# A hybrid two-layer decoder trunk on one core: other look-ups in PEER, wide u products throughout, an un-normed first third in the conv mixer, and an earlier split of an output slab

## The chip, the cores and the metric

One core of one Trainium2 chip. The metric is the time of one execution in microseconds of device time, and the median over several runs stands for a kernel. Engines are named as in the profile: PE (TensorE matmuls; PEld its weight loads), DVE (VectorE), ACT (ScalarE), POOL (GpSimd), SP (SyncE, which issues the transfers).

## What is computed

256 tokens of width 1024 pass two layers: a gated short convolution or an attention, each followed by a PEER expert retrieval, with a norm ahead of each and one at the end.

```python
def reference(x, ...):
    for i in range(DEPTH):                      # DEPTH = 2
        hn = rms_norm(x, norm_mix[i])
        if i % N_MIXERS == 0:
            x = x + short_conv_mixer(hn, conv_w_in[j], conv_w[j], conv_w_out[j])
        else:
            x = x + moba_mixer(hn, attn_w_qkv[j], attn_w_o[j])
        x = x + peer_ffn(rms_norm(x, norm_ffn[i]), peer_w_q[i], peer_k1[i], peer_k2[i], peer_u[i], peer_v[i])
    return rms_norm(x, norm_final)

def short_conv_mixer(h, w_in, conv_w, w_out):
    b_gate, c_gate, z = jnp.split(h @ w_in, 3, axis=-1)
    ...                                         # causal convolution of c_gate * z, width 3
    return (b_gate * u_conv) @ w_out

# peer_ffn, per chunk of 128 tokens, 8 heads
        v1, i1 = lax.top_k(s1, PEER_TOPK)       # 16 of 128 keys, twice
        v2, i2 = lax.top_k(s2, PEER_TOPK)
        top_s, top_pos = lax.top_k(cand, PEER_TOPK)     # 16 of the 256 sums
        e_idx = jnp.take_along_axis(cidx, top_pos, axis=-1)
        g = jax.nn.softmax(top_s, axis=-1)
        a = jax.nn.gelu(jnp.einsum('td,thkd->thk', xc, u_emb[e_idx]), approximate=False)
        return jnp.einsum('thk,thkd->td', g * a, v_emb[e_idx])
```

All values are float32; the 16384 experts of a layer have one row in u_emb and one in v_emb.

## The kernel before, in words

The order of the work on every engine is written out by hand. All weights pass as a row of tiles ("items") of 128x1024: 24 of conv_w_in in the order c gate, z, b gate, 8 of conv_w_out, then for layer 0's PEER 8 of w_q, 128 of u and 128 of v, then the same for the second layer with 24 of attn_w_qkv and 8 of attn_w_o. Three buffers each hold an item raw, split into a rounded part `hi` (ACT, L171) and the rest `lo` (DVE or POOL, L176); `halved` names the items whose POOL split runs as two halves. The activations are split alike (XH, XL), and each product is the sum of hi·XH, hi·XL and lo·XH. `issue` starts an item's transfer on SP as soon as the item three places ahead of it is split; `prefetch(n)` transposes u items to n+3 (DVE, L157) and splits to n+2 ahead of item n's matmuls (`next_item`).

PEER multiplies with all 16384 rows of u and v. A u item gives 128 rows for 256 tokens; from item WIDE on, hi multiplies XH and XL as one operand of 512 columns (L965) into a whole bank, ACT copies one half out (L1144), DVE adds the other (`both`, L1134) and ACT applies the gelu; below WIDE = 16, three products of 256 columns (L967, L968, L971) sum up in half a bank. Four banks are used in turn, so item k+4 waits for the add of item k's pair.

Beside the first 64 u items, DVE makes the look-ups from a list of side work: `add(cost, ...)` puts one operation on it, and after each item `run_side(1.62)` issues as many as the saved-up credit pays for; `pause()` ends a round. Per half of the tokens (i = 0, 1): top-k of the scores and of the sums, then for each of 128 picks its two key numbers, by comparing the pick's row and column with thresholds (`is_ge`, `is_equal` into `hot`), multiplying by the table `vp` and summing over 16 places, with folds (`fold`, L1029) by 8, 4 and 2 and a last add. The side list has line L215 for all that is called through `add`. Later side work (L1174, L1182, L1196) turns the list into gates.

The start: x is loaded, its squares summed, the norm applied, x transposed on PE and split, and only then the 8 c-gate items are multiplied (`mm_wstat`, L545), then z and b gate. Dummy matmuls (`warm`, L299) keep PE at work meanwhile. After the last b-gate item, DVE multiplies the gated result (L683), ACT rounds it (L684) and the 8 conv_w_out items follow (L558); the second of these is split on POOL. In attention, the v third begins with two items taken together, bank by bank (`mm_bank`, L565 to L567).

## Time and profile before

| what | value |
|---|---|
| median of 3 runs | 1809.76 us (1808.52 to 1813.9) |
| the profiled execution | 1812.88 us, of which its span is 1811.1 us |
| busy: PE, DVE, ACT, POOL | 99%, 76%, 50%, 39% of the span |
| granted clock of PE, mean | 0.995 of 2.4 GHz |
| read from HBM | 315.83 MB, 176 GB/s over the span |
| chain that ended last | PE 87%, DVE 7%, DMA 3% |

The busy share says how long an engine had some instruction in flight. Since matmuls overlap, PE's share stays near 100% where it issues more slowly too; its pace is read from the starts of its instructions.

### The profile page before, as it was taken

Reading aid. Unit: us, or ns where it says so; the run is one execution under the profiler, and the core shown is the slowest. Engines: PE = TensorE matmul, PEld = TensorE weight load, DVE = VectorE, ACT = ScalarE, POOL = GpSimd, SP = SyncE. Lnnn points to the kernel's source line nnn. Section 1 sums busy time; section 2 is a strip of 40 time slices with the busy share of each in tenths; the row PEclk is TensorE's granted clock in tenths of the full one; section 3 lists DMA queues with packets and bytes.
Section 4 is the critical chain, followed back from the end, with each engine's and each line's share of the span. In section 5 each row is a group of like instructions: output and inputs, shape, how many; then the busy total and the mean of one; then the engine's idle time right before and its main releaser. Section 6 shows DMA issues by size and latency. Waiting matters only on the chain.

```text
span 1811.1 us, 30954 instructions
## 1 busy us (share of the span) xinstructions
PE 1791.1 (99%) x11217; PEld 1536.6 (85%) x11217; DVE 1370.7 (76%) x2251; ACT 906.8 (50%) x1153; POOL 700.2 (39%) x553
## 2 busy tenths in 40 slices
PE   9999999999999999999999999999999999999998
PEld 8979988888888888888878799888888888888886
DVE  4648899888888887555566488998888898875555
ACT  5455555554554444544454555565455544445443
POOL 1047888888720000000220388988888200000000
PEclk9999999999999999999999999999999999999999
DMA  7566566656556556766562665665565565657664
GB/s 206 157 196 197 167 176 174 187 166 176 171 157 182 168 171 185 228 193 196 172 181 83 174 198 168 182 179 174 172 175 164 158 186 169 176 176 230 193 193 138
DMA packets 204576, 321.06 MB, mean 177 GB/s; under 512 B 26221, under 2 KB 157317, under 8 KB 203910
## 3 DMA queue, kind: packets, MB, share of 16 engines
q1 hardware_dynamic: 202006, 312.33, 58.4%
q10 hardware_dynamic: 2416, 6.75, 1.1%
q8 instruction: 88, 1.44, 0.3%
q14 instruction: 66, 0.54, 0.1%
HBM read 315.83 MB, written 3.15 MB: 176 GB/s over the span
## 4 chain that ended last, share of the span: by engine, by line
PE 87%; DVE 7%; DMA 3%; issue 1%; ACT 1%; POOL 1%; SPq 1%; DVEq 0%; ACTq 0%; POOLq 0%
PE psum L558 40%; PE psum L965 19%; PE psum L971 11%; PE psum L1189 4%; PE psum L545 3%; DVE tr L157 2%; DVE big L215 2%; PE psum L968 2%; PE psum L967 2%; PE psum L591 2%; DMA raw<-in_peer_u_dram 1%; DVE lo L176 1%; PE psum L1003 1%; POOL lo L176 1%; PE psum L567 1%
## 5 line engine op out<-in xcount | busy, mean ns | idle before, releaser
L176 POOL TENSOR_TENSOR lo<-tr,hi 128x512 fp32r<-128x512 f32 x496 | 632.5, 1310 | 120.1 <-ACT hi L171 120.1
L171 ACT ACTIVATE hi<-raw 128x1024 fp32r<-128x1024 f32 x331 | 350.0, 1060 | 452.4 <-PE psum L558 362.7
L176 DVE TENSOR_TENSOR lo<-raw,hi 128x1024 fp32r<-128x1024 f32 x312 | 382.7, 1228 | 253.6 <-ACT hi L171 247.4
L558 PE MATMUL psum<-hi,x 128*128 128x512 f32 x2208 | 553.2, 392 | 0.7 <-ACT hi L171 0.7
L558 PEld LDWEIGHTS psum<-hi,x 128*128 128x128 f32 x2208 | 409.0, 188 | 82.6 <-ACT hi L171 1.1
L965 PE MATMUL psum<-x,hi 128*128 128x512 f32 x1792 | 458.9, 397 | 5.2 <-DVE big L1134 5.2
L965 PEld LDWEIGHTS psum<-x,hi 128*128 128x128 f32 x1792 | 323.2, 190 | 64.6 <-issue 4.2
L157 DVE STREAM_TRANSPOSE tr<-raw 128x1024 f32<-128x1024 f32 x256 | 315.6, 1233 | 43.2 <-DMA raw<-in_peer_u_dram 26.6
L171 ACT ACTIVATE hi<-tr 128x1024 fp32r<-128x1024 f32 x256 | 270.7, 1059 | 144.5 <-DVE tr L157 134.1
L558 PE MATMUL psum<-lo,x 128*128 128x512 f32 x1104 | 295.1, 389 | 0.4 <-POOL lo L176 0.4
L971 PEld LDWEIGHTS psum<-x,lo 128*128 128x128 f32 x2048 | 279.5, 191 | 18.0 <-POOL lo L176 0.2
L176 POOL TENSOR_TENSOR lo<-raw,hi 128x1024 fp32r<-128x1024 f32 (+1 forms) x31 | 58.3, 1904 | 599.7 <-ACT hi L171 558.1
L971 PE MATMUL psum<-x,lo 128*128 128x256 f32 x2048 | 289.2, 283 | 0.0
L558 PEld LDWEIGHTS psum<-lo,x 128*128 128x128 f32 x1104 | 207.1, 188 | 43.8 <-POOL lo L176 0.8
L1144 ACT ACTIVATE big<-psum 128x512 f32<-128x512 f32 x112 | 66.8, 596 | 165.6 <-PE psum L971 165.4
L1289 POOL TENSOR_TENSOR big<-xbuf,big 128x256 f32<-128x256 f32 x2 | 1.4, 732 | 383.4 <-DVE rstd L348 383.4
L1134 DVE TENSOR_TENSOR big<-psum,big 128x512 f32<-128x512 f32 x112 | 77.2, 689 | 72.3 <-ACT big L1144 72.0
L1174 DVE TENSOR_TENSOR xbuf<-psum,eT 128x1536 f16<-128x1536 f16 x128 | 119.8, 936 | 10.2 <-PE psum L1189 10.2
L1196 DVE SCALAR_TENSOR_TENSOR big<-psum,big 128x512 f32<-128x512 f32 x128 | 86.5, 677 | 3.1 <-PE psum L1189 3.1
L1182 DVE TENSOR_TENSOR xbuf<-xbuf,psum 128x1024 f16<-128x1024 f16 x128 | 85.8, 671 | 1.3
L1189 PEld LDWEIGHTS <-xbuf 128*128 128x128 f16 x2048 | 68.5, 97 | 19.5 <-issue 15.7
L1189 PE MATMUL psum<-xbuf 128*128 128x64 f16 x2048 | 83.7, 193 | 0.0
(173 smaller groups left out, 1451.0 us busy)
## 6 DMA issues: line engine op xcount, KB each, us to landing
raw<-in_peer_u_dram SPq DMA_DIRECT2D x1024, 128.0 KB, 2.9
raw<-in_peer_v_dram SPq DMA_DIRECT2D x256, 512.0 KB, 3.7
raw<-in_conv_w_in_dram SPq DMA_DIRECT2D x96, 128.0 KB, 2.7
raw<-in_attn_w_qkv_dram SPq DMA_DIRECT2D x96, 128.0 KB, 2.6
raw<-in_peer_w_q_dram SPq DMA_DIRECT2D x64, 128.0 KB, 3.1
raw<-in_conv_w_out_dram SPq DMA_DIRECT2D x8, 512.0 KB, 3.9
raw<-in_attn_w_o_dram SPq DMA_DIRECT2D x8, 512.0 KB, 3.6
x_dram<-xbuf ACTq DMA_DIRECT2D x2, 1024.0 KB, 4.8
```

What stands on the lines that cost most here:

```text
L157: dve.transpose(TR[m % 3].rearrange("p b (g i) -> p g b i", g=4), RAW[m % 3].rearrange("p (g m) -> p g m", m=256))
L171: act.activation(HI[m % 3], src, AF.Copy)
L176: eng.tensor_sub(LO[m % 3][:, c], src[:, c], HI[m % 3][:, c])
L558: pe.matmul(banks[j], x[:, j // 2 * 128:j // 2 * 128 + 128], w[:, j % 2 * 512:j % 2 * 512 + 512], start=(first and p == 0), stop=(last and ...
L965: pe.matmul(o, w, X2[:, b], start=(b == 0), stop=False, skip_group_check=True)
L971: pe.matmul(o[:, 0:256], lo[:, b * 128:b * 128 + 128], XH[:, b], start=False, stop=(b == 7), skip_group_check=(o.shape[-1] == 512))
L1134: dve.tensor_tensor(a, halves(k, 0), a, op=OP.add)
L1144: act.activation(A[:, k - 1:k + 1], halves(k, 1), AF.Copy)
L1174: dve.tensor_tensor(HOT[s % 2].rearrange("p b (r k) t -> p b r k t", r=3), numbers[:, None, None].to_broadcast([128, TOK // 2, 3, 64, 2]), ...
L1182: dve.tensor_tensor(OHG[s % 2], one_hot[:, None].to_broadcast([128, 2, TOK // 2, 64, 2]), gate_rows[:, s, :, :, None, :].to_broadcast([128 ...
L1189: pe.matmul(o, pairs[:, t // 2, :, t % 2], OHG[s % 2][:, a, t // 2, :, t % 2], start=(a == 0), stop=(a == 1))
L1196: dve.scalar_tensor_tensor(w, banks[s % 3].rearrange("p (t k) -> p k t", k=64), 1.0 / GSC, w, op0=OP.mult, op1=OP.mult)
```

## The change

- **Wide u products:** WIDE is 0 in both layers, so all u items take the 512-column form.
- **Look-ups:** tables hold each entry once, not twice; the places of a pick lie side by side in `hot`, the compares (`hits`) write pairs, and two TENSOR_REDUCE in place of three folds and an add form the sums. The 128x128 subtract and others that read two operands from SBUF get one of them through PSUM. Costs on the side list change, and a `pause()` follows.
- **First third of the conv:** x is transposed un-normed, scaled by the gain on the way out of PSUM (`chunk`), and multiplied with the c-gate items. The token factors come later (`norm_behind`), as a row R that two matmuls spread; the eight chunks are rescaled for the z and b thirds (`normed`), and the c gate gets R when it leaves PSUM. Half of x is loaded on ACT's queue ahead of the weights, the other half on SP's behind three items.
- **Second output slab:** its split is called behind the first gated copy.
- **Attention:** two more items are split in halves.

```diff
-WIDE = (16, 16)
+WIDE = (0, 0)
...
     def load_x(i, h):
-        c = slice(h * 512, h * 512 + 512)
-        sp.dma_start(x_in[:, i * D + h * 512:i * D + h * 512 + 512], x[0, i * 128:(i + 1) * 128, c])
+        (sp if h else act).dma_start(x_in[:, (2 * h + i) * 512:(2 * h + i) * 512 + 512].rearrange("p (q r) -> p q r", q=4),
+                     x[0, i * 128:(i + 1) * 128].rearrange("p (q r) -> p q r", q=4)[:, :, 128 * h:128 * h + 128])
...
-    warm(WARM)
-    spread_gain(hi4[2:4])
+    warm(WARM - 8)
+    gT = sb.tile([128, 8], F32, name="gT")
+    pe.transpose(lo4[3][:, 0:8], gr8, ident[0:8, 0:8])
+    dve.tensor_copy(gT, lo4[3][:, 0:8])
+    warm(11)
...
+    def chunk(c):
+        bk = hi4[c % 4][:, c // 4 * 256:c // 4 * 256 + 256]
+        for i in range(2):
+            pe.transpose(bk[:, i * 128:i * 128 + 128], XT[i][:, c * 128:c * 128 + 128], ident)
+        act.activation(XH[:, c], bk, AF.Copy, scale=gT[:, c:c + 1])
+        dve.scalar_tensor_tensor(XL[:, c], bk, gT[:, c:c + 1], XH[:, c], op0=OP.mult, op1=OP.subtract)
+    def normed(c):
+        v = scratch(3 * D + c % 2 * 256, 256)
+        pool.tensor_tensor(v, XH[:, c].bitcast(F32), XL[:, c].bitcast(F32), op=OP.add)
+        dve.tensor_tensor(v, v, R, op=OP.mult)
+        act.activation(XH[:, c], v, AF.Copy)
+        dve.tensor_sub(XL[:, c], v, XH[:, c])
     def norm_in():
...
+        for i in range(2):
+            kept(i, 0)
+        chunk(0)
         split_to(0)
+        for c in (1, 2, 3):
+            chunk(c)
+        warm(4)
+    def norm_behind(b):
+        if b == 1:
+            for i in range(2):
+                kept(i, 1)
+                squares(i, 0)
+                begun(i)
+        elif b == 2:
+            for c in range(4, 8):
+                chunk(c)
+        elif b == 3:
...
+            for i in range(2):
+                root(i)
+                dve.tensor_scalar(scratch(i * 128, 128), ident, rstd[:, i:i + 1], -0.5, op0=OP.mult, op1=OP.mult)
+            late_consts()
+        elif b == 4:
+            for i in range(2):
+                pe.matmul(hi4[0][:, i * 128:i * 128 + 128], ones, scratch(i * 128, 128), start=True, stop=True)
+            load_gain(norm_ffn, 0)
+            load_keys(0)
+        elif b > 4:
+            if b == 5:
+                dve.tensor_copy(R, hi4[0][:, 0:256])
+            normed(b - 5)
...
             next_item(mm_wstat(lo4, b), 1.0)
+            norm_behind(b)
         drain_side()
-        for j in range(4):
-            act.activation(cT[:, 2 * j:2 * j + 2].rearrange("p c t -> p (c t)"), lo4[j], AF.Copy)
         for b in range(8):
             next_item(mm_wstat(hi4, b))
+            if b < 5:
+                normed(b + 3)
+            if 1 < b < 6:
+                s = slice(2 * b - 4, 2 * b - 2)
+                dve.tensor_tensor(cT[:, s], lo4[b - 2].rearrange("p (c t) -> p c t", t=256),
+                                  R[:, None].to_broadcast([128, 2, 256]), op=OP.mult)
...
             if j:
                 out_lo(j - 1)
+            else:
+                split_to(n + 1)
...
                 on_pool.update(range(n + 15, n + 20))
+                halved.update((n + 16, n + 17))
...
+        def hits(i, c, ends, op):
+            dve.tensor_tensor(hot[i][:, 8 * c:8 * c + 8].rearrange("p h n (a r) -> p (h n) a r", r=2),
+                              picks[:, c, :, None].to_broadcast([128, 128, 8, 2]),
+                              ends.rearrange("p (a r) -> p a r", r=2)[:, None].to_broadcast([128, 128, 8, 2]), op=op)
...
-            add(0.5, dve.tensor_tensor, gg[:, i], ts[:, i], ts[:, i, :, 0:1].to_broadcast([128, 8, 16]),
+            add(0.3, dve.tensor_copy, side1, ts[:, i])
+            add(0.3, dve.tensor_tensor, gg[:, i], side1, ts[:, i, :, 0:1].to_broadcast([128, 8, 16]),
                 op=OP.subtract)
...
-            add(0.3, dve.tensor_copy, pf.rearrange("p s h n -> p (s h n)"), room(128, 256))
+            add(0.6, dve.tensor_copy, pf, room(128, 256)[:, :, None].to_broadcast([128, 256, 2]))
...
-            for n in (8, 4, 2):
-                add(0.3 + 0.14 * n, fold, i, n)
-            add(0.6, dve.tensor_tensor, e12[:, i].rearrange("p s (h n) -> p (s h) n", h=8), hot[i][:, :, 0],
-                hot[i][:, :, 1], op=OP.add)
+            add(1.2, hits, i, 0, st16, OP.is_ge)
+            add(1.2, hits, i, 1, io16, OP.is_equal)
+            add(2.3, dve.tensor_tensor, hot[i], hot[i], values[:, :, None].to_broadcast([128, 16, 16, 16]), op=OP.mult)
+            for c in range(2):
+                add(1.7, dve.tensor_reduce, e12[:, i, c].rearrange("p (h n) -> p h n", h=8),
+                    hot[i][:, 8 * c:8 * c + 8], axis=AX.X, op=OP.add)
+        pause()
```

DVE in layer 0, the tail of the second half's look-up, first before and then with the change. Transposes mark the u items; L1134 and L1160 are the same add, L215 and L217 the side list.

```order
L157 STREAM_TRANSPOSE tr_71<-raw_68 128x4x8x32
L1134 TENSOR_TENSOR big<-psum,big 128x512
L157 STREAM_TRANSPOSE tr_69<-raw_66 128x4x8x32
L215 TENSOR_TENSOR big<-big,psum 128x4096
L157 STREAM_TRANSPOSE tr_70<-raw_67 128x4x8x32
L1029 TENSOR_TENSOR big<-big 128x16x128
L1029 TENSOR_TENSOR big<-big 128x16x64
L1029 TENSOR_TENSOR big<-big 128x16x32
L1134 TENSOR_TENSOR big<-psum,big 128x512
L157 STREAM_TRANSPOSE tr_71<-raw_68 128x4x8x32
L215 TENSOR_TENSOR big<-big 128x256
```

```order
L157 STREAM_TRANSPOSE tr_71<-raw_68 128x4x8x32
L217 TENSOR_TENSOR big<-big,psum 128x4096
L1160 TENSOR_TENSOR big<-psum,big 128x512
L157 STREAM_TRANSPOSE tr_69<-raw_66 128x4x8x32
L217 TENSOR_REDUCE big<-big 128x128
L157 STREAM_TRANSPOSE tr_70<-raw_67 128x4x8x32
L1160 TENSOR_TENSOR big<-psum,big 128x512
L157 STREAM_TRANSPOSE tr_71<-raw_68 128x4x8x32
L217 TENSOR_REDUCE big<-big 128x128
```

Three folds stood between a transpose and the add; now one reduce stands between two transposes, and the multiply comes one item earlier. In the first half the change has the multiply alone, a reduce ahead of the add, the second reduce, and then the next half's five preparations ahead of the add:

```order
L217 TENSOR_TENSOR big<-big,psum 128x4096
L157 STREAM_TRANSPOSE tr_69<-raw_66 128x4x8x32
L217 TENSOR_REDUCE big<-big 128x128
L1160 TENSOR_TENSOR big<-psum,big 128x512
L157 STREAM_TRANSPOSE tr_70<-raw_67 128x4x8x32
L217 TENSOR_REDUCE big<-big 128x128
L157 STREAM_TRANSPOSE tr_71<-raw_68 128x4x8x32
L217 CAST psum<-big 128x256
L217 CAST big<-psum 128x256
L217 TENSOR_TENSOR xbuf<-psum,big 128x8x15
L217 COPY psum<-big 128x128
L217 TENSOR_TENSOR big<-big,psum 128x8x16
```

Here the two reduces follow each other in neighbouring items. PE at the start of the program with the change (L390 the transposes of x, L297 dummies, L568 the c-gate products, L436 the two matmuls that spread the token factors):

```order
L390 MATMUL psum<-ident,xbuf 128x128 x8
L297 LDWEIGHTS ident
L297 MATMUL psum<-ident 128x256
...
L568 MATMUL psum<-x_78,hi_72 128x256 x16
L568 MATMUL psum<-x_78,lo_75 128x256 x8
L568 MATMUL psum<-x_78,hi_73 128x256 x8
L568 MATMUL psum<-x_78,lo_76 128x256 x8
L568 MATMUL psum<-x_78,hi_73 128x256 x8
L568 MATMUL psum<-x_78,hi_74 128x256 x8
L568 MATMUL psum<-x_78,lo_77 128x256 x8
L568 MATMUL psum<-x_78,hi_74 128x256 x8
L390 MATMUL psum<-ident,xbuf 128x128 x8
```

The first four of x's eight chunks are transposed ahead of the products, the other four behind the third item.

## Rows read from the trace of the kernel before

**Rows 1.** The page's part 1: busy us (share of the span), instructions.

```profile
PE 1791.1 (99%) x11217; PEld 1536.6 (85%) x11217; DVE 1370.7 (76%) x2251; ACT 906.8 (50%) x1153; POOL 700.2 (39%) x553
```

**Rows 2.** Timeline of PE, narrow u tiles: start us, us, engine, line, operation.

```profile
144.71 1.12 PE L971 MATMUL psum<-x,lo 128*128 128x256 f32 x8
147.59 1.12 PE L971 MATMUL psum<-x,lo 128*128 128x256 f32 x8
```

**Rows 3.** Timelines of DVE and PE, wide u tiles, first half's look-up.

```profile
201.43 0.69 DVE L1134 TENSOR_TENSOR big<-psum,big 128x512 f32<-128x512 f32 x1
...
206.19 2.00 PE L965 MATMUL psum<-x,hi 128*128 128x512 f32 x8
...
271.80 0.68 DVE L1134 TENSOR_TENSOR big<-psum,big 128x512 f32<-128x512 f32 x1
...
273.23 2.00 PE L965 MATMUL psum<-x,hi 128*128 128x512 f32 x8
...
276.02 2.00 PE L965 MATMUL psum<-x,hi 128*128 128x512 f32 x8
```

**Rows 4.** Timeline, layer 0, second half's look-up ([idle before <- what ended it]).

```profile
284.92 10.09 POOL L176 TENSOR_TENSOR lo<-tr,hi 128x512 fp32r<-128x512 f32 x8
...
290.93 4.22 DVE L215 TENSOR_TENSOR big<-big 128x128 f32<-128x128 f32 x1
...
292.78 2.00 PE L965 MATMUL psum<-x,hi 128*128 128x512 f32 x8
...
310.50 4.57 DVE L1029 TENSOR_TENSOR big<-big 128x2048 f16<-128x2048 f16 x3
...
315.82 3.62 PE L965 MATMUL psum<-x,hi 128*128 128x512 f32 x8 [1.91 <-DVE big L1134]
...
320.23 2.00 PE L965 MATMUL psum<-x,hi 128*128 128x512 f32 x8
```

**Rows 5.** Timeline of PE, layer 1, the same eight tiles' first and last.

```profile
1202.83 2.00 PE L965 MATMUL psum<-x,hi 128*128 128x512 f32 x8
...
1230.14 2.17 PE L965 MATMUL psum<-x,hi 128*128 128x512 f32 x8
```

**Rows 6.** Timeline, start of the program.

```profile
9.26 1.06 ACT L171 ACTIVATE hi<-raw 128x1024 fp32r<-128x1024 f32 x1
...
10.40 5.03 POOL L176 TENSOR_TENSOR lo<-raw,hi 128x512 fp32r<-128x512 f32 x3 [9.33 <-DMA raw<-in_conv_w_in_dram]
...
12.09 2.07 PE L545 MATMUL psum<-x,hi 128*128 128x256 f32 x8 [0.69 <-ACT x L377]
...
24.43 1.12 PE L545 MATMUL psum<-x,lo 128*128 128x256 f32 x8
```

**Rows 7.** Stretches: busy us of PE, PEld, DVE, ACT, POOL; PEclk, DMA share, GB/s.

```profile
6.00:9.00 3.00, 2.87 (x13) 1.40 (x12) 2.33 (x9) 1.96 (x6) 0.00 (x0) 0.92 1.05 275
9.00:12.00 3.00, 2.10 (x9) 1.10 (x7) 2.93 (x6) 1.80 (x4) 1.60 (x2) 0.50 0.82 224
```

**Rows 8.** Timeline of PE, second item of the conv's output projection.

```profile
88.15 2.11 PE L558 MATMUL psum<-hi,x 128*128 128x512 f32 x8 [0.71 <-ACT hi L171]
90.64 1.19 PE L558 MATMUL psum<-lo,x 128*128 128x512 f32 x4 [0.38 <-POOL lo L176]
```

**Rows 9.** Timeline, first two items of attention's v third.

```profile
941.51 4.73 POOL L176 TENSOR_TENSOR lo<-raw,hi 128x1024 fp32r<-128x1024 f32 x2 [1.27 <-ACT hi L171]
...
943.93 0.50 PE L567 MATMUL psum<-lo,x 128*128 128x512 f32 x1 [1.72 <-POOL lo L176]
```

**Rows 10.** Groups by line and form, DVE: busy us, mean ns | idle before.

```profile
L157 DVE STREAM_TRANSPOSE tr<-raw 128x1024 f32<-128x1024 f32 x256 | 315.6, 1233 | 43.2 <-DMA raw<-in_peer_u_dram 26.6
L215 DVE TENSOR_TENSOR big<-psum,big 128x2048 f16<-128x2048 f16 x8 | 9.5, 1184 | 0.0
L215 DVE TENSOR_TENSOR big<-big,psum 128x4096 f16<-128x4096 f16 x4 | 9.0, 2248 | 0.0
L215 DVE TENSOR_REDUCE big<-big 128x16 f32<-128x256 f32 x2 | 0.8, 403 | 0.0
```

134 lines of the change are left out of this document (46 added, 88 removed).

## The prediction

> **What bounds the kernel now.** I read the page first: TensorE (PE) is busy 99% of the span [rows 1], so a change gains only where it gives PE less to do, lets it start earlier, or removes a place where PE issues nothing or runs at the lower clock. The busy share hides such places, because the ends of matmuls are modelled. So I read PE's timeline next and measured from start to start. In the u loop a tile's products take 2.88 us while they are written as 24 narrow matmuls [rows 2] and 2.79 us in the wide form (from 273.23 to 276.02 [rows 3]). Where tiles follow each other at 2.79 nothing is lost. Then I looked for longer steps.
>
> The largest are in the second half of PEER's look-ups. VectorE (DVE) must run the add of line 1134 before PE may reuse the pair's banks. Usually that add ends 4.06 us ahead of the matmul (201.43 + 0.69 against 206.19); in the first half's look-up the margin shrinks to 0.75 (271.80 + 0.68 against 273.23) [rows 3]. In the second half it is gone [rows 4]: the 128x128 subtract with both inputs in SBUF takes 4.22 us from 290.93, ending as GpSimd's run of eight splits ends (284.92 + 10.09 = 295.01); at 310.50 three folds take 4.57 us, and PE waits 1.91 us at 315.82 and then needs 3.62 us for eight matmuls instead of 2.00. From 292.78 to 320.23 eight tiles take 27.45 us instead of 8 x 2.79 = 22.32: **5.1 us lost**. In layer 1 the same eight tiles take 1230.14 - 1202.83 = 27.31: **5.0 us** [rows 5].
>
> Three smaller places: the start, where PE's first product begins at 12.09 [rows 6] at a granted clock of 0.50, that is 1.2 GHz [rows 7]; the first tiles of the conv's output projection, with waits of 0.71 and 0.38 us [rows 8]; and the v third of attention, with 1.72 us [rows 9].
>
> **The change, part by part.**
>
> *Wide u products.* WIDE goes from 16 to 0 in both layers, so 16 tiles a layer go from 2.88 to 2.79 us [rows 2, 3]: 32 x 0.09 = **-2.9 us**. In exchange DVE gets seven more adds a layer (0.69 each [rows 3]) and ScalarE as many copies. The cover is DVE's spare time there: the same slots with the same top-k operations and the add already exist from tile 17 on, and they keep the full 4.06 us of margin, as at 201.43 [rows 3], so I cost it at nothing. Without that cover each add would cost at most its own 0.69, 9.7 us in all.
>
> *Look-ups.* What PE sees is DVE's lag behind 2.79 us a tile, which hurts only beyond 4.06. I price a tile's slot in the new order from [rows 10], from start to start (some 0.07 less than the durations): transpose 1.16, compare 1.12, multiply 2.18, the line-1134 add 0.60. The sum over pairs (two folds by 8 and 4, one by 2, and a last add) becomes two TENSOR_REDUCE over 128x2048. No row shows that size: at the rate of the 128x2048 compare it would be 1.18 us, at the rate of the 128x256 reduce (403 ns, 1.57 ns an element) 3.2. I take 2.4: from the reduce of 256 (403 ns) to the add of 512 (0.69 us), which also reads f32 at its plain pace, an element costs 1.12 ns, and 1792 elements more make 403 + 2007 ns. Then in the first half's tail: multiply 1.16 + 2.18 = 3.34; reduce and add 1.16 + 2.4 + 0.60 = 4.16; reduce 3.56; the next half's preparation and add, five small operations of 0.3 to 0.4, 3.54. Above 2.79 that is 0.55 + 1.37 + 0.77 + 0.75 = 3.4 us of lag: a margin of 0.6 at the tightest add. At 3.2 the lag is 5.0 and PE waits 1.0 us a layer; at 1.18 the margin is 3. The point of decision is 2.7 us a reduce.
>
> In the second half the 4.22 us subtract becomes a copy into PSUM and a subtract from it, each under the 0.69 of an operation four times as long, and no operation with two SBUF inputs stands between 54 and 63. The order there puts only an add between the two reduces, so the lag stays under 2 us even at 3.2. So 5.1 + 5.0 comes back less what I leave for small waits, 0.25 a layer: **-9.6 us**. The wider copies of positions (512 instead of 256 outputs) are inside these slots. What is late next: nothing I see up to the listing, which moves one tile later with its PE transposes unchanged.
>
> The trace's folds took 4.57 us beside GpSimd. The Trainium skill says the opposite of this edit: "VectorE: DVE Perf Modes", section "Rules for kernel authors", expects `tensor_reduce` at 1x and calls it the slowest DVE operation to be restructured away, and its table "Side-by-side" gives about 2.29 us for 2048 elements at 1x and 1.22 at 2x. By that page two reduces are an estimated 4.6 us and undisturbed folds 2.8, so the edit would add 1.8 us a half and give back no wait. The row decides against it here: 4.57 is what three folds cost in place.
>
> *Start.* The norm leaves the path ahead of the first matmul: of 12.09 us, what remains is the load of half of x and the first weight tile, two copies, a transpose and one ScalarE copy. DMA moves 275 GB/s in 6 to 9 us [rows 7]; x and the first tile, 1.57 MB, are there by 9.26, where ScalarE begins on the tile [rows 6]: 5.7 us of transfer behind 3.5 of issue and latency. Half of x and a tile are 1.05 MB, 3.8 us, so the tile lands near 7.3, and ScalarE splits it in halves of 0.6: first product at 8.0 instead of 12.09. GpSimd then paces: it splits the first three tiles, the first in two halves of 1.3 us (with the second tile 5.03 [rows 6]), the others whole at 2.4 (4.73 for two [rows 9]); from 7.9 that is 2.6, then from the second tile's hi copy at 10.7 two of 2.4, done at 15.5. The third tile ends near 17.7, the eight transposes of the other half of x (0.9) and a wait of 0.5 for its copies follow, and the fourth tile's lo products run at 20.1 instead of 24.43: 4.3. Against it: the 24-row transpose comes later (0.24), two matmuls spread the token factors (0.22), and PE waits for DVE's and ScalarE's chain of roots ahead of them, 0.4 by the order of their work: **-3.4 us**. The loads move too: half of x goes out on ScalarE's queue ahead of its table load, the weights pass the other half on SyncE's queue (it is wanted 5 us after it lands), and the gain and the keys, three issues of some 0.4 us, now sit between two hi copies of ScalarE behind tile 4, which has over a microsecond to spare there. Bounds: -5 if nothing waits; -1 if x in pieces of 512 bytes halves the load rate (3.8 us more), and PE drops to 1.2 GHz again. The rescaling of eight chunks behind tiles 5 to 12 puts 0.8 us on DVE, 0.4 on ScalarE and 0.7 on GpSimd a tile beside a 1.23 us split, within 2.88, and each chunk is ready two tiles before its use; its last subtract waits some 0.5 us for ScalarE with the next tile's split behind it, which has a tile to spare: nothing. ScalarE's four evictions of 0.6 become DVE products in tiles 10 to 13, used 3 tiles later: nothing.
>
> *Second output slab.* Its hi copy runs behind the first gated copy instead of the fourth, three copies and 3 us earlier; its lo split on GpSimd then ends near 87.5, before it is wanted at 89. PE's two waits of 0.71 and 0.38 go, and with them the slow restart behind each (90.64 lies 0.65 past 88.15 and eight matmuls of 0.23 [rows 8]), some 0.25 each: **-1.6**; at least -0.7 if a load is late, and the later gated copies, each 1.06 later, are wanted from 90 on.
>
> *Attention.* The two tiles' lo splits in halves let PE go on at 942.9, not 943.93 [rows 9]: half of the 2.37 us split, **-1.1**; bounds 0 and -1.8.
>
> **Sum.** 2.9 + 9.6 + 3.4 + 1.6 + 1.1 = 18.6. The profiled execution is 1812.88 us (span 1811.1), which gives 1794.3; it lies 3.1 above the median of the runs, 1809.76, and against that the forecast is 1791.2, rounded **1791.0 us**.
>
> **The rivals.**
> 1. *Reduces too slow.* Each reduce at 3.2 us or more: PE waits 1.0 us a layer at the first half's tail and, as at 315.82, pays up to 1.6 for the lower clock: 5 us of the 9.6 is given back, 1796. For: the margin in the first half is only 0.6 by my sum. Against: the 403 ns row contains a fixed cost. Chance 0.12. (The page of the Trainium skill named above has the reduce as the slowest operation, which speaks for this rival; by its 2.29 us it would not come.)
> 2. *The start gives little.* The first tile lands with x, PE waits idle and starts at 1.2 GHz, and GpSimd's chain is as late as now: 1793.5 to 1794. For: 512-byte pieces and one DMA system for both. Chance 0.2.
> 3. *Slower than before.* The compares and the multiply, rewritten with pairs as the inner dimension, lose their packed rate. At the f32 rate of the line-1134 add (0.69 us for 512) two compares and a multiply of 8192 elements a half take 11.0 us instead of 4.6: a lag of 3.4 + 6.4 = 9.8 in the first halves and 8.4 in the second, so 5.7 and 4.3 us beyond 4.06, with 1.6 of clock each: 26.4 us, where 10.1 is lost now. With the other gains (9.0) that is 1809.8 - 9.0 + 16.3 = 1817.1. It decides where the four halves lose 19.1 together, at a lag of 7.2 us. Against: the compares already broadcast both operands and take 1184 ns for 2048 elements [rows 10], and the new ones keep neighbours in pairs. Chance 0.03.
> 4. *The edits don't bite*: the waits return elsewhere, as on GpSimd, and only the wide products and the attention halves stay: 1805.8. Against: PE's other stretches step at their bare pace. Chance 0.03.
>
> **How the numbers follow.** The forecast's case has 0.62. The range 1786 to 1799 takes in -5 at the start, the upper bounds of slab and attention (-3), rivals 1 and 2 and part of both together, and leaves out rivals 3 and 4 and a base that is off by some 3 us. About 0.3% (5.4 us) can be told from no change: faster 0.93, same 0.04, slower 0.03.
>
> **What would show it.** First product near 8.0 us and the fourth tile's lo products near 20; all u tiles without side matmuls at 2.79 from the first; TENSOR_REDUCE rows of 2.2 to 2.7 us; no wait of PE on the line of the add in either layer and a clock of 1.00 there; no wait on the second slab; the v third's wait under 0.8. I am wrong if a reduce exceeds 2.7 and PE waits for the add, if the first product is later than 9.5, or if the compares exceed 1.3 us.

## The result, and the profile after

The changed kernel takes **1798.15 us** (median of 4 runs, 1796.98 to 1799.56) against 1810.51 us of the kernel before in the same comparison (4 runs, 1808.52 to 1813.9): ratio 0.9931, 95% interval 0.9917 to 0.9946. The forecast was 1791.0, in a range of 1786 to 1799.

| what | after |
|---|---|
| the profiled execution | 1798.12 us, of which its span is 1796.3 us |
| busy: PE, DVE, ACT, POOL | 99%, 77%, 51%, 39% of the span |
| granted clock of PE, mean | 0.999 of 2.4 GHz |
| read from HBM | 315.83 MB, 178 GB/s over the span |
| chain that ended last | PE 91%, DVE 3%, DMA 3% |

The busy time of PE fell by 11.2 us against [rows 1], with 256 matmuls fewer. The page's part 1:

```profile
PE 1779.9 (99%) x10961; PEld 1518.3 (85%) x10961; DVE 1377.8 (77%) x2287; ACT 915.4 (51%) x1178; POOL 701.2 (39%) x563
```

The spans differ by 1811.11 - 1796.34 = 14.8 us. Where they came from is read from the same matmul in both traces: its start after, minus its start before. The table gives this for all kernels that it needs (negative: ahead of before, in us; "u" are layer 0's tiles of that stage; PEER's head is the first transposes of its norm; the end of the thirds and the tile columns go by the last matmul there).

| kernel | first product | 4th item | 9th item | end of the thirds | PEER's head | u, tile 16 | u, tile 60 | scores of attention | layer 1, tile 60 | end |
|---|---|---|---|---|---|---|---|---|---|---|
| changed | -3.45 | -2.88 | -1.76 | -0.88 | -2.95 | -3.81 | -8.91 | -8.61 | -14.49 | -14.77 |
| e1 start only | -3.04 | -2.30 | -1.43 | -0.85 | -1.06 | -0.58 | -2.10 | -1.88 | -2.12 | -2.13 |
| e5 look-ups only | 1.28 | 1.51 | 1.51 | 1.52 | 1.77 | 1.81 | -3.30 | -3.07 | -8.12 | -8.41 |
| e6 subtract only | 0.40 | 0.38 | 0.38 | 0.39 | 0.20 | 0.29 | -4.81 | -4.63 | -9.10 | -9.41 |
| e9 old subtract | -3.45 | -2.88 | -2.01 | -1.03 | -3.00 | -3.90 | -5.77 | -5.50 | -8.07 | -8.36 |
| e10 no rewrite | -2.94 | -2.48 | -1.44 | -0.76 | -2.83 | -3.69 | -8.79 | -8.85 | -14.93 | -15.20 |
| e2 folds back | -2.81 | -2.25 | -1.38 | -0.78 | -2.64 | -3.50 | -7.10 | -6.62 | -12.59 | -12.85 |
| e7 no early slab | -3.18 | -3.21 | -2.14 | -0.89 | -0.87 | -1.79 | -6.89 | -7.09 | -12.89 | -13.16 |
| e3 early | -3.69 | -5.31 | -2.70 | -1.49 | -3.01 | -4.87 | -9.96 | -10.55 | -16.97 | -17.26 |
| e4 early, order | -3.23 | -4.85 | -2.10 | -2.09 | -4.16 | -6.03 | -11.12 | -11.35 | -17.67 | -17.96 |
| e8 roots, taps | -3.22 | -4.84 | -3.69 | -4.27 | -5.79 | -7.65 | -12.75 | -12.64 | -18.87 | -19.13 |
| e11 tables early | -2.90 | -4.52 | -3.65 | -4.22 | -6.00 | -7.85 | -12.95 | -14.16 | -19.80 | -20.09 |

One warning: e5 and e6 have the start of before, letter for letter, and their first product comes 1.28 and 0.40 us later. The start alone varies by a microsecond from one execution to another, so in its columns only larger differences count.

**Look-ups.** From tile 16 to tile 60 the changed kernel gains 5.1 us in layer 0, and 4.9 between the same tiles in layer 1. The timeline of the second half, answering to [rows 4]:

```profile
286.42 0.28 DVE L217 COPY psum<-big 128x128 f32<-128x128 f32 x1
286.74 0.29 DVE L217 TENSOR_TENSOR big<-psum,big 128x128 f32<-128x128 f32 x1
...
288.97 2.00 PE L992 MATMUL psum<-x,hi 128*128 128x512 f32 x8
...
301.58 2.24 DVE L217 TENSOR_REDUCE big<-big 128x128 f32<-128x2048 f16 x1
...
306.63 2.24 DVE L217 TENSOR_REDUCE big<-big 128x128 f32<-128x2048 f16 x1
...
311.32 2.00 PE L992 MATMUL psum<-x,hi 128*128 128x512 f32 x8
```

From 288.97 to 311.32 eight tiles take 22.35 us, 2.79 each: nothing is lost, where 27.45 were taken before. The operation of 4.22 us has become two of under 0.3. The groups in layer 0 alone, which answer to [rows 10]:

```profile
L217 DVE TENSOR_REDUCE big<-big 128x128 f32<-128x2048 f16 x4 | 9.0, 2242 | 0.0
...
L1056 DVE TENSOR_TENSOR big<-psum,big 128x2048 f16<-128x2048 f16 x4 | 4.8, 1194 | 0.0
...
L217 DVE TENSOR_TENSOR big<-big,psum 128x4096 f16<-128x4096 f16 x2 | 4.5, 2247 | 0.0
```

A reduce takes 2.24 us (2.4 was taken, 2.7 was the point of decision); compares and multiply kept their pace. The page "VectorE: DVE Perf Modes" of the Trainium skill, section "Side-by-side", has about 2.29 us for 2048 elements at 1x; the trace agrees with 2.24.

**Start.** PE's timeline, with the ScalarE copy that starts late, answering to [rows 6]:

```profile
7.22 0.98 PE L390 MATMUL psum<-ident,xbuf 128*128 128x128 f32 x7 [1.07 <-DVE xbuf L383]
...
8.63 2.21 PE L568 MATMUL psum<-x,hi 128*128 128x256 f32 x16
...
13.67 1.22 PE L568 MATMUL psum<-x,lo 128*128 128x256 f32 x8 [0.69 <-POOL lo L178]
...
16.08 1.06 ACT L173 ACTIVATE hi<-raw 128x1024 fp32r<-128x1024 f32 x1 [3.00 <-DMA raw<-in_conv_w_in_dram]
...
19.46 1.38 PE L390 MATMUL psum<-ident,xbuf 128*128 128x128 f32 x8 [0.74 <-DVE part L334]
...
21.63 1.12 PE L568 MATMUL psum<-x,lo 128*128 128x256 f32 x8
```

The first product comes at 8.63 instead of 12.09, the fourth item's lo products at 21.63 instead of 24.43, at a granted clock of 1.00, that is 2.4 GHz, where [rows 7] has 0.50 in 9 to 12 us. But three waits (1.07, 0.69, 0.74 us) stand in between, and of 3.45 us ahead 1.76 are left at the ninth item and 0.88 at the end of the thirds. Two stretches of the same timeline show how the rest went, VectorE's first and then PE's:

```profile
38.46 0.43 DVE L402 TENSOR_TENSOR x<-big,x 128x256 fp32r<-128x256 f32 x1 [0.48 <-ACT x L401]
39.41 1.38 DVE L178 TENSOR_TENSOR lo<-raw,hi 128x1024 fp32r<-128x1024 f32 x1 [0.52 <-ACT hi L173]
40.71 0.41 DVE L400 TENSOR_TENSOR big<-big 128x256 f32<-128x256 f32 x1
41.61 0.43 DVE L402 TENSOR_TENSOR x<-big,x 128x256 fp32r<-128x256 f32 x1 [0.48 <-ACT x L401]
42.55 1.38 DVE L178 TENSOR_TENSOR lo<-raw,hi 128x1024 fp32r<-128x1024 f32 x1 [0.52 <-ACT hi L173]
...
77.48 1.22 PE L568 MATMUL psum<-x,hi 128*128 128x256 f32 x8 [0.83 <-ACT hi L173]
```

While chunks are rescaled, VectorE's steps are 42.55 - 39.41 = 3.14 us an item, against PE's 2.88. It isn't busy all that time: it waits 0.48 us for ScalarE's rounding of the chunk and then 0.52 for ScalarE's hi copy of the next item, which stands behind that rounding on ScalarE. So splits, and the loads that wait for them, fall behind; PE feels it only at 77.48.

**Attention.** The same timeline at the start of the k and of the v third:

```profile
894.33 1.98 ACTq L308 DMA_DIRECT2D big<-in_peer_k_dram  x1
...
897.34 1.06 ACT L173 ACTIVATE hi<-raw 128x1024 fp32r<-128x1024 f32 x1 [2.65 <-DMA raw<-in_attn_w_qkv_dram]
...
909.67 0.50 PE L590 MATMUL psum<-lo,x 128*128 128x512 f32 x1 [0.74 <-DVE lo L178]
...
910.81 0.50 PE L590 MATMUL psum<-lo,x 128*128 128x512 f32 x1 [0.17 <-DVE lo L178]
...
935.35 0.49 PE L590 MATMUL psum<-lo,x 128*128 128x512 f32 x1 [0.63 <-POOL lo L178]
```

The v third's wait is 0.63 instead of 1.72 us [rows 9], 1.1 us won. At the k third, where nothing waited before, two waits (0.74 and 0.17, and some 0.5 of slow restart) take it away again in this execution.

### The profile page after: what moved, and what is told of

It is laid out like the page before. It is cut to its first block, busy times and chain, and to the rows that moved or that the text cites. A ratio compares the mean times of both kernels' runs of the same rounds, so it can differ in the third digit from the quotient of the medians.

```text
span 1796.3 us, 30521 instructions
## 1 busy us (share of the span) xinstructions
PE 1779.9 (99%) x10961; PEld 1518.3 (85%) x10961; DVE 1377.8 (77%) x2287; ACT 915.4 (51%) x1178; POOL 701.2 (39%) x563
## 3 DMA queue, kind: packets, MB, share of 16 engines
q8 instruction: 86, 1.41, 0.3%
HBM read 315.83 MB, written 3.15 MB: 178 GB/s over the span
## 4 chain that ended last, share of the span: by engine, by line
PE 91%; DVE 3%; DMA 3%; ACT 2%; issue 1%; POOL 1%; SPq 1%; ACTq 0%; DVEq 0%; POOLq 0%
PE psum L581 39%; PE psum L992 27%; PE psum L998 14%; PE psum L1215 4%; PE psum L614 2%; DVE lo L178 2%; PE psum L568 1%; ACT hi L173 1%; DMA raw<-in_conv_w_in_dram 1%; PE psum L1030 1%; POOL lo L178 1%; PE psum L590 0%; PE psum L589 0%; PE psum L588 0%; DMA raw<-in_peer_w_q_dram 0%
## 5 line engine op out<-in xcount | busy, mean ns | idle before, releaser
L173 ACT ACTIVATE hi<-raw 128x1024 fp32r<-128x1024 f32 (+1 forms) x332 | 349.9, 1057 | 436.4 <-PE psum L581 364.2
L992 PE MATMUL psum<-x,hi 128*128 128x512 f32 x2048 | 521.3, 396 | 0.0
L992 PEld LDWEIGHTS psum<-x,hi 128*128 128x128 f32 x2048 | 368.3, 189 | 66.6
L178 POOL TENSOR_TENSOR lo<-raw,hi 128x512 fp32r<-128x512 f32 (+1 forms) x33 | 58.7, 1808 | 566.3 <-ACT hi L173 526.7
L1170 ACT ACTIVATE big<-psum 128x512 f32<-128x512 f32 x128 | 76.5, 598 | 177.5 <-PE psum L998 177.3
L1160 DVE TENSOR_TENSOR big<-psum,big 128x512 f32<-128x512 f32 x128 | 88.0, 688 | 75.2 <-ACT big L1170 74.5
L1200 DVE TENSOR_TENSOR xbuf<-psum,eT 128x1536 f16<-128x1536 f16 x128 | 119.8, 936 | 10.2 <-PE psum L1215 10.2
```

The costliest lines, as they stand in the source:

```text
L173: act.activation(HI[m % 3][:, w], src[:, w], AF.Copy)
L178: eng.tensor_sub(LO[m % 3][:, c], src[:, c], HI[m % 3][:, c])
L992: pe.matmul(o, w, X2[:, b], start=(b == 0), stop=False, skip_group_check=True)
L1160: dve.tensor_tensor(a, halves(k, 0), a, op=OP.add)
L1170: act.activation(A[:, k - 1:k + 1], halves(k, 1), AF.Copy)
L1200: dve.tensor_tensor(HOT[s % 2].rearrange("p b (r k) t -> p b r k t", r=3), numbers[:, None, None].to_broadcast([128, TOK // 2, 3, 64, 2]), ...
```

## The experiments

Theory after the traces: the look-ups paid as predicted, but by which part is open (the subtract, or the folds); the start was mis-sized because VectorE, ScalarE and the loads don't follow PE forward. The kernel before was timed beside each group of runs.

**e1: the start alone.** The kernel before with `load_x`, `chunk`, `norm_behind`, `normed` and the conv loops of the change, and nothing else:

```diff
 WIDE = (16, 16)
...
+        for b in range(8):
+            next_item(mm_wstat(lo4, b), 1.0)
+            norm_behind(b)
```

> The kernel before with the new start of the conv alone (un-normed first third, loads, late rescaling; nothing else of the change). Theory A: the start is worth little because what it wins at the first product is given back: PE is 3.4 us ahead at the first product, 1.8 ahead at the ninth item, and 0.9 ahead at the end of the conv's three thirds, since the loop of VectorE and ScalarE over the rescaled chunks steps at 3.15 us against PE's 2.88; about 1809.6 in all. Rival B (the prediction): 3.4 us stay, 1807.1.

Measured: 1811.16 against 1812.03 us, ratio 0.9996 (0.9987 to 1.0006). Theory A: PE is 3.04 ahead at the first product, 1.43 at the ninth item, 0.85 at the end of the thirds. What the span has beyond that (2.13) came at tile 60 of layer 0, which the start doesn't touch. PE waits there as in [rows 4], but the eight matmuls behind the wait take 2.08 us instead of 3.62, and the granted clock differs. The timeline of e1's PE:

```profile
315.26 2.08 PE L990 MATMUL psum<-x,hi 128*128 128x512 f32 x8 [1.91 <-DVE big L1159]
```

The same stretch in the profiled execution of the kernel before and then in e1 (busy us of PE, PEld, DVE, ACT, POOL; granted clock, DMA share, GB/s):

```profile
315.00:318.00 3.00, 2.18 (x5) 1.82 (x6) 2.96 (x7) 1.06 (x2) 1.20 (x1) 0.62 0.03 9
...
315.00:318.00 3.00, 2.74 (x15) 2.43 (x16) 2.97 (x6) 1.62 (x3) 1.13 (x2) 1.00 0.20 52
```

After the same wait of 1.91 us the clock was partly at 1.2 GHz in one execution and at 2.4 GHz in the other. So 1.6 of the 5.1 us that the kernel before lost there belongs to its profiled execution and not to every one.

**e2: folds back.** In the changed kernel:

```diff
-            for c in range(2):
-                add(1.7, dve.tensor_reduce, e12[:, i, c].rearrange("p (h n) -> p h n", h=8),
-                    hot[i][:, 8 * c:8 * c + 8], axis=AX.X, op=OP.add)
+            for n in (8, 4, 2):
+                add(0.3 + 0.14 * n, fold, i, n)
+            add(0.6, dve.tensor_tensor, e12[:, i].rearrange("p s (h n) -> p (s h) n", h=8), hot[i][:, :, :, 0],
+                hot[i][:, :, :, 1], op=OP.add)
```

> The changed kernel with the sums over 16 places made by three folds and a last add again (in the new layout), in place of two reduces; all else as changed. Theory A: folds with both inputs in SBUF run beside GpSimd's splits at some 4.6 us for three, PE waits for the add again in the second halves, and 1.9 us of wait and 1.6 of lower clock come back a layer: about 1805. Rival B: the folds are cheap (2.8 us for three and less than two reduces of 2.24), PE waits nowhere, 1798. In either case the copy and subtract through PSUM stay short.

Measured: 1799.7 us, ratio 0.9933 (0.9917 to 0.995); its span is 1.9 us longer than the changed kernel's. Neither theory: not 7 us, and not nothing. Its groups in layer 0, folds (L1062) and last add:

```profile
L1062 DVE TENSOR_TENSOR big<-big 128x512 f16<-128x512 f16 x2 | 3.5, 1766 | 0.1
L1062 DVE TENSOR_TENSOR big<-big 128x2048 f16<-128x2048 f16 x2 | 3.3, 1655 | 0.0
L217 DVE TENSOR_TENSOR big<-big 128x256 f32<-128x256 f16 x2 | 2.9, 1461 | 0.0
L1062 DVE TENSOR_TENSOR big<-big 128x1024 f16<-128x1024 f16 x2 | 2.1, 1044 | 0.0
```

Together 5.9 us a half instead of 2 x 2.24, and the smallest fold is the longest: its time is waiting. The one wait of PE that this costs in layer 0 stands in the first half, not the second, in PE's timeline:

```profile
271.16 2.08 PE L992 MATMUL psum<-x,hi 128*128 128x512 f32 x8 [1.27 <-DVE big L1165]
```

So the second half no longer depended on the folds, and something else had made the 5.1 us. That left the subtract.

**e6 and e5: the subtract alone, and all of the look-ups alone.** e6 is the kernel before with one edit, and e5 the kernel before with the whole new look-ups:

```diff
-            add(0.5, dve.tensor_tensor, gg[:, i], ts[:, i], ts[:, i, :, 0:1].to_broadcast([128, 8, 16]),
+            add(0.3, dve.tensor_copy, side1, ts[:, i])
+            add(0.3, dve.tensor_tensor, gg[:, i], side1, ts[:, i, :, 0:1].to_broadcast([128, 8, 16]),
                 op=OP.subtract)
```

> The kernel before with one edit: the 128x128 subtract of the top sums reads one operand through PSUM (a copy into PSUM, then the subtract); folds, last add and order as before. Theory A: putting the folds back into the changed kernel lost only 1.9 us, so most of the look-ups' gain is the end of the 4.22 us subtract and the place of the operations: 3 to 7 us faster than before over two layers, the two operations under 0.35 us each. Rival B: the folds in front of the add decide, and the wait of 1.9 us at that tile stays in both layers: under 2 us faster.

> The kernel before with the new look-ups alone (single tables, places side by side, two reduces, copies through PSUM, costs and the pause). Theory A: the 10.2 us that the look-ups give back in the changed kernel's trace are theirs alone, so this is 10 us faster than before and PE waits for the add of a tile pair nowhere; first halves' margins at about 0.6 us or more. Rival B: a part of them needs the wide products in the first 16 tiles or the other phase of the loads, and 7 or less are seen.

Measured in one comparison, against 1813.31 us: e6 1803.44, ratio 0.9949 (0.9932 to 0.9966); e5 1803.25, ratio 0.9948 (0.9931 to 0.9964). **Changing one operation of 128x128 was enough for the whole gain of the look-ups**, 10 us. From tile 16 to 60 of layer 0 e6 gains 5.10, e5 5.11. Theory A of both, though e6 expected 3 to 7.

**e9 and e10: the same question within the changed kernel.** e9 is the changed kernel with the subtract of before (e6's edit backwards). e10 is the changed kernel with the look-ups of before, tables, folds, order and all, and only e6's edit in them.

> The changed kernel with one part undone: the 128x128 subtract of the top sums reads both operands from SBUF again, in one operation. Theory A: this one operation, held by GpSimd's run of splits, carried what the look-ups lost before, and the reduces do not make up for it: PE waits for the add again and 3 to 5 us a layer come back, 1804 to 1808. Rival B: before, it took the subtract and the folds together to use up the 4.06 us of margin; with reduces in place of the folds the subtract alone is absorbed, and this stays within 1 us of the changed kernel, 1798 to 1799.

> The changed kernel with the look-ups of before (double tables, three folds, a last add, the costs and order of before), of which only the subtract is changed to go through PSUM. Theory A: as in the kernel before with the subtract alone changed, nothing waits in the look-ups, so the reduces and the pairs are worth nothing in this kernel: 1798 +- 1. Rival B: with wide products in the first 16 tiles and the other phase of the loads the folds run beside GpSimd again and 1.9 us or more are lost, as with the folds put back: 1800 or more.

Measured against 1812.05 us: e9 1800.62 (seven runs from 1798.05 to 1804.56), ratio 0.9944 (0.9928 to 0.996); e10 1797.75, ratio 0.9932 (0.9912 to 0.9952), as the changed kernel's. e10's expectation A held: beside the new subtract, the reduces, the pairs and the single tables gain nothing in time. Timeline of e9, layer 0:

```profile
276.83 13.87 POOL L178 TENSOR_TENSOR lo<-tr,hi 128x512 fp32r<-128x512 f32 x11
...
286.28 4.56 DVE L217 TENSOR_TENSOR big<-big 128x128 f32<-128x128 f32 x1
...
292.45 2.08 PE L992 MATMUL psum<-x,hi 128*128 128x512 f32 x8 [0.61 <-DVE big L1159]
...
311.58 2.08 PE L992 MATMUL psum<-x,hi 128*128 128x512 f32 x8 [1.41 <-DVE big L1159]
```

The subtract ends at 290.84, when GpSimd's run of eleven splits ends (290.70), just as before (295.15 after 295.01 [rows 4]). In this profiled run, the slowest of the seven, the second half loses 3.2 us a layer at a clock of 1.00. That is little less than the 3.5 us which the kernel before lost in layer 0 without the 1.6 at the lower clock. But the seven runs reach from theory B's times to theory A's, and by the medians the old subtract costs 2.5 us here (1800.62 against 1798.15) and 9.9 beside the folds (1813.31 against e6's 1803.44). So the reduces do soften what the old subtract costs, by an amount that varies from run to run; with the new subtract they have nothing to soften. e10's timeline, with the folds (L1057) beside GpSimd:

```profile
286.29 0.28 DVE L217 COPY psum<-big 128x128 f32<-128x128 f32 x1
286.60 0.29 DVE L217 TENSOR_TENSOR big<-psum,big 128x128 f32<-128x128 f32 x1
...
289.09 2.00 PE L993 MATMUL psum<-x,hi 128*128 128x512 f32 x8
...
303.39 3.75 DVE L1057 TENSOR_TENSOR big<-big 128x2048 f16<-128x2048 f16 x2
...
311.44 2.00 PE L993 MATMUL psum<-x,hi 128*128 128x512 f32 x8
```

Two folds take 3.75 us and still eight tiles take 22.35. The margins say why. They are worked out from the traces of layer 0: from the end of the add to the start of the matmul that takes its banks, in us, by the pair's second tile; 0.15 means that PE waited.

| pair of tile | before | e6 | changed | e2 | e9 |
|---|---|---|---|---|---|
| 43 | 0.75 | 1.68 | 1.13 | 0.15 | 1.18 |
| 51 | 0.15 | 4.05 | 3.49 | 2.59 | 0.15 |
| 53 | 0.15 | 3.51 | 3.02 | 2.13 | 0.15 |
| 55 | 1.94 | 4.06 | 2.43 | 1.53 | 0.15 |
| 57 | 0.15 | 0.90 | 2.97 | 0.58 | 0.15 |

The subtract stands ahead of the add of pair 51 and eats the whole margin there; six tiles later it isn't yet won back, and so the folds at pair 57 show up as PE's longest wait. Without the old subtract they leave 0.90 (e6) and cost nothing.

**e7: without the early slab.**

```diff
             if j:
                 out_lo(j - 1)
-            else:
-                split_to(n + 1)
```

> The changed kernel without the early split of the second output slab (its hi copy again behind the last gated copy). Theory A: PE waits again about 0.7 us for the hi copy and 0.4 for the lo split in the second item of the output projection and the start of the head is 1.6 us later than in the changed kernel: 1799.8. Rival B: with the changed kernel's earlier items nothing waits there and it stays at 1798.2.

Measured: 1800.07 us, ratio 0.9932 (0.9915 to 0.9948), 1.9 above the changed kernel's median; at PEER's head it is 2.1 behind the changed kernel. Theory A, with both waits as in [rows 8]:

```profile
87.24 2.14 PE L581 MATMUL psum<-hi,x 128*128 128x512 f32 x8 [0.69 <-ACT hi L173]
...
89.72 1.19 PE L581 MATMUL psum<-lo,x 128*128 128x512 f32 x4 [0.34 <-POOL lo L178]
```

**e3: copies and squares early, the second lo split on VectorE.** In the changed kernel:

```diff
-    on_pool, on_dve, halved = set(range(3)), set(), {0}
+    on_pool, on_dve, halved = {0, 2}, set(), {0}
...
-        if b == 1:
+        if b == 0:
             for i in range(2):
                 kept(i, 1)
                 squares(i, 0)
                 begun(i)
+        elif b == 1:
+            for i in range(2):
+                squares(i, 1)
+            for i in range(2):
+                mean(i)
```

> The changed kernel with three moves at the start: the lo split of the second item on VectorE instead of GpSimd; the copies and first squares of the other half of x one item earlier, ahead of the fourth item's lo split; the second squares and square roots two items earlier. Theory A: the waits of 0.95 us (second item's lo), 1.24 us (the transposes behind the third item) and most of the 0.3 at the two matmuls of the factors go, so PE is 4.2 us ahead of before at the ninth item instead of 1.8; but the chunk loop takes it back and the end of the thirds moves by under 1 us: about 1797.5. Rival B: it is all kept, 1795.8.

Measured: 1796.19 us, ratio 0.992 (0.9905 to 0.9936). Neither theory whole: the end of the thirds moves by 0.6 us as in A, but the ninth item is 2.7 us ahead of before and not 4.2. The fourth item is 2.4 us earlier than in the changed kernel, the ninth 0.9: the two waits went, but the factors' roots were still late (below), and the taps still waited.

**e4: the rescaling in two steps.** On top of e3, `normed` does addition and product, and `renewed` ScalarE's rounding and the last subtract, one item later, behind the next split:

```diff
+    def renewed(c):
+        v = scratch(3 * D + c % 2 * 256, 256)
+        act.activation(XH[:, c], v, AF.Copy)
+        dve.tensor_sub(XL[:, c], v, XH[:, c])
```

> The same with the rescaling of a chunk cut in two: addition and product behind one item, ScalarE's rounding and the last subtract behind the next item's split. Theory A: VectorE no longer waits twice 0.5 us an item, the loop steps at 2.88 or less, and the gain at the start reaches the end of the thirds: 1794 to 1795, the fastest. Rival B: loads hold the items in any order, and it stays with the kernel before this edit within 0.5 us.

Measured: 1794.93 us, ratio 0.9912 (0.9898 to 0.9925). Theory A: from the ninth item to the end of the thirds nothing is lost (-2.10 to -2.09). The longest waits of PE that remained in the thirds, in its timeline:

```profile
25.51 0.49 PE L441 MATMUL psum<-big 128*128 128x128 f32 x2 [0.90 <-DVE big L437]
26.47 0.49 PE L441 MATMUL psum<-big 128*128 128x128 f32 x2 [0.47 <-DVE big L437]
```

**e8: roots earlier, taps spread.** On top of e4:

```diff
         elif b == 2:
-            for c in range(4, 8):
+            chunk(4)
+            for i in range(2):
+                root(i)
+                dve.tensor_scalar(scratch(i * 128, 128), ident, rstd[:, i:i + 1], -0.5, op0=OP.mult, op1=OP.mult)
+            for c in range(5, 8):
                 chunk(c)
...
-            next_item(mm_wstat(lo4, b), 2.4, b < 7)
+            next_item(mm_wstat(lo4, b), 1.3, b < 7)
```

> The kernel with early copies and the rescaling cut in two, and two edits more: the roots ahead of three of the four chunk roundings behind the third item, and the credit for the taps of the convolution 1.3 us an item instead of 2.4, so that they spread over eight items. Theory A: the wait of 1.6 us at the two matmuls of the factors goes, and the waits at 76 to 78 us, caused by 4.27 us of VectorE work an item, go too: PE is 3.7 us ahead of before at the ninth item instead of 2.1, and 3.5 at the end of the thirds; 1793. Rival B: the work is only moved: the late taps hold the gate's product after the last item, and the end of the thirds gains under 0.5 us.

Measured: **1793.72 us, ratio 0.9898 (0.9882 to 0.9915)**, an interval below the changed kernel's 0.9917 to 0.9946, and its slowest run (1794.32) is below the changed kernel's fastest (1796.98): this version beats both kernels. Both waits of e4 are gone, as PE's timeline shows in the same place,

```profile
24.47 0.61 PE L442 MATMUL psum<-big 128*128 128x128 f32 x4
```

and PE is 3.69 ahead at the ninth item and 4.27 at the end of the thirds, where the changed kernel had 1.76 and 0.88.

**e11 and e12: the tables and keys early, and x on two queues.** e11 is e8 with the four small loads of attention's start (the cosines, the sines and two of keys) issued in layer 0's v stage. e12 is e11 with the two first blocks of x on two queues. In both kernels these tables lie where two of the v stage's 128 tiles still read their activations, so layer 0's output is computed from other numbers there, with the same instructions and transfers: they tell of time only.

```diff
-        act.dma_start(cosT, rope_cos.rearrange("(b p) i -> p b i", p=128))
-        act.dma_start(sinT[:, :, 0:32], rope_sin.rearrange("(b p) i -> p b i", p=128))
...
-        load_keys(1)
...
                 load_gain(norm_mix if l == 0 else norm_final, 1 - l)
+                if l == 0:
...
+                    load_keys(1)
```

> The kernel with roots and taps moved, and one edit more: attention's rotary tables and the second layer's keys, four loads of 832 packets in all on ScalarE's queue, go out in layer 0's v stage instead of in the first third of attention. Theory A: these loads make the next weight tile land 3.8 instead of 2.6 us after its issue and hold SyncE's queue, VectorE's splits come 1 us late and PE waits 1.1 us at the start of the k third; that goes and nothing replaces it: 1792.5, the fastest. Rival B: the wait has another cause (the chain of roots on VectorE ahead of the two splits), and it stays: 1793.7.

> The same with the two first blocks of x issued on two queues at once (ScalarE's and SyncE's) and the gain's small load behind them on ScalarE's. Theory A: the second block lands 0.6 us earlier, ahead of the weight tile's pieces, the wait of 0.85 to 1.6 us ahead of its transposes shrinks, and the first product starts 0.3 to 0.5 us earlier: 1792.1. Rival B: the weight tile is later by as much, or the gain's load holds the chunk, and the first product does not move or comes later.

Measured: e11 1792.66 us, ratio 0.9901 (0.9884 to 0.9918); e12 1793.12, ratio 0.9905 (0.9888 to 0.9922). The medians don't separate them from e8; the traces do. In e8 PE waits at the k third, in its timeline:

```profile
905.66 0.50 PE L598 MATMUL psum<-lo,x 128*128 128x512 f32 x1 [0.57 <-DVE lo L178]
906.79 0.50 PE L598 MATMUL psum<-lo,x 128*128 128x512 f32 x1 [0.17 <-DVE lo L178]
```

In e11 PE waits nowhere in the k third and is 1.5 us further ahead at the scores, of which 1.0 is left at the end. So the small loads cause that wait; theory A. How long it is varies between kernels with the same instructions there: the first key load's issue (1.98 us in the changed kernel's trace above) took 1.41 us in e3, 1.51 in e7 and 1.66 in e10, with a first wait of PE of 0.18, 0.28 and 0.43 us. Why it is long in these kernels and 0.49 us in the kernel before, where the same loads stand at the same distance and PE doesn't wait, stays open. In e12 the first product comes 1.2 us earlier than in e11, little more than the start varies by itself, and at the ninth item 0.1 of it is left: PE waits 0.83 us in the sixth item instead.

## Why the prediction was right, and where it was not

The measured time lies in the range, 0.85 us below its upper end. The sum was 18.6 us; the spans of the two profiled executions give 14.8: 10.2 of the look-ups, 2.8 of the wide products, 2.1 of the slab and 0.9 of the start, less 0.3 in attention up to the scores and 0.5 and 0.4 lost elsewhere. The other 3.1 us of the miss are the base: the working subtracted from the median of three runs, 1809.76, which the later comparisons put at 1810.5 to 1813.3 us, while the losses had been read from an execution of 1812.88 us. By the medians of the first comparison the gain is 12.4 us. That the range held is in part luck: it was made to leave out a base that is off by some 3 us, and such a base came together with a start that gave little.

- **Look-ups: predicted 9.6, measured 10.2** (5.1 and 5.1 to the end). The size was right, and so were the reduce (2.24 for 2.4), the tightest margin (1.13 for 0.6) and the compares. The reason was half wrong. The step "the 4.22 us subtract becomes a copy into PSUM and a subtract from it" was enough for all of it (e6, e10). The step beside it, that the sum over pairs by reduces had to be fast enough, with a point of decision of 2.7 us, weighed an edit that beside the new subtract moves nothing and beside the old one only softens the loss (e9). The row that misled is the folds' 4.57 us right in front of PE's longest wait: that wait was the end of a lag which began 20 us earlier. Also, 1.6 of the 5.1 us in layer 0 (3.62 for 2.00) and some 1.4 of the 5.0 in layer 1 were the lower clock behind that wait, which e1's execution lacks in layer 0: the prediction took them for a fixed part of the loss.
- **The rule against reduces.** Undisturbed folds at 2.8 us, the prediction's estimate from the page "VectorE: DVE Perf Modes" of the Trainium skill, section "Side-by-side", never came: three folds and the last add took 5.9 us a half in e2 and some 4.3 in e10, beside 4.48 for two reduces. The rule would have misjudged the edit by little, and the row that the prediction set against it, 4.57, decided as little.
- **Start: predicted 3.4, measured 1.8 at the ninth item and 0.9 at the end of the thirds; alone it can't be told from no change (e1).** Rival 2 came in its size, by another mechanism: the clock stayed at 1.00, but the chain behind was late. At the fourth item's lo products 4.3 was expected and 2.8 came. "First product at 8.0" was 8.63: the second block of x let the transposes wait 1.07 us. "A wait of 0.5 for its copies" was 1.24 with the restart: the copies stood behind the fourth lo split, and its tile landed only at 16 us. The 0.86 that follow (the 24-row transpose, the two matmuls, the chain of roots) were 1.04 here; PE's wait at the two matmuls, under 0.3 us here, grew to 1.2 and 1.4 us once PE came earlier (e3, e4). And "its last subtract waits some 0.5 us for ScalarE ... which has a tile to spare: nothing" missed a second wait of 0.52 that follows from it, 3.14 us an item against 2.88, which cost the 0.9 at the end of the thirds. With these mended (e8) the start gives 3.7 at the ninth item, and 4.3 at the end of the thirds together with the spread taps.
- **Second slab: predicted 1.6, measured 2.1** at PEER's head, 1.9 in the medians (e7): 1.7 at the slab itself, as priced, and 0.4 some 14 us later.
- **Attention: predicted 1.1, measured 1.1 at the v third, and lost again at the k third**, 26 us earlier, so that PE is 0.3 us less ahead at the scores than at tile 60. In e3, e7 and e10, with shorter waits at the k third, it is 0.1 to 0.6 us further ahead there, so the loss isn't fixed. The prediction looked for nothing late there, though VectorE's splits had no margin left: in the trace of before PE's step at that place is already 0.08 us longer than its neighbours.
- **Wide products: predicted 2.9, measured 2.8.** From the first u tile to tile 16 PE gains 1.4 us in each layer: sixteen steps, and where nothing else stands between two tiles a step takes 2.79 instead of 2.88 us, as priced.
- **Not foreseen:** 0.5 us ahead of layer 0's u stage, where the transposes of the queries at 126.40 us now wait 0.38 us for ScalarE's copies, and 0.4 in attention's output projection, where PE waits 0.28 us for a split of VectorE at 1004.85 us.
- **The other rivals.** 1 and 3 didn't come (2.24 us a reduce, 1.19 a compare). 4 came in part: two waits did return elsewhere.

## What to carry to other kernels

Where a stage loses time by a lag against a fixed margin, follow the margin from pair to pair back to where it first shrinks; the operation in front of the longest wait may cost nothing by itself. An edit that starts PE earlier gives only what the engines and loads behind it can follow: count each one's step per item against PE's, and its waits for others in that step too, not its busy time alone. Losses that are read from one execution belong to that execution: subtract them from its own time, and ask which of them, such as a drop of the clock, another execution would not have. And when two edits aim at one loss, try each alone: one may be enough.

## What the runs showed of the hardware

In the second half's look-up, a VectorE operation of 128x128 with both inputs in SBUF took 4.22 us before and 4.56 us in e9, and both times it ended within 0.15 us of the end of GpSimd's run of splits; with one input in PSUM it took 0.29. The same operation in the first half's look-up took only 0.67 us, though GpSimd went on splitting, in the timelines of VectorE and GpSimd before:

```profile
247.89 0.67 DVE L215 TENSOR_TENSOR big<-big 128x128 f32<-128x128 f32 x1
...
247.12 5.12 POOL L176 TENSOR_TENSOR lo<-tr,hi 128x512 fp32r<-128x512 f32 x4 [0.54 <-ACT hi L171]
```

It ended at 248.56, 0.15 us after the first of those four splits (248.41). So the operation ended just behind a split in both halves, but in the second half three more splits of 1.3 us started and ended within the 4.22. The page "SBUF — State Buffer" of the Trainium skill, section "Who interferes with whom", has it that a VectorE instruction with two SBUF inputs contends with a GpSimd instruction that reads SBUF, and calls what they share an exclusive lock; the trace agrees that it waits. Why it got in after one split in one place and after four in the other isn't shown by any run.

The kernel before varies more than the others: its runs in one comparison spread over 8.8 us (1806.51 to 1815.32 in 12 runs), e9's over 6.5, e1's over 3.6, while the changed kernel, e2 to e8 and e10 each stay within 3. A part of it goes with the clock: over the last three comparisons, its executions with a mean granted clock of 0.999 took 1806.5 to 1808.9 us and those with 0.994 or 0.995 took 1809.9 to 1815.3. The clock doesn't explain e9, whose seven runs all had 0.999. That the old subtract makes the spread fits e9 but is not shown: e6, which differs from the kernel before by the subtract alone, has too few runs (2.7 us in 4, against 3.8 in 7 of the kernel before beside it).
